# A hybrid encoder trunk on one core: sink columns copied a period later, the first token tile transformed ahead in the Fourier layer, four weight loads placed a product later

## The chip, the cores and the metric

The kernel runs on one NeuronCore of a Trainium2 chip. Five engines work at once, each through its own list of instructions in order: TensorE (PE, matmuls and transposes; its weight loads are shown apart as PEld), VectorE (DVE), ScalarE (ACT), GpSimd (POOL) and SyncE (SP, which here only issues DMA transfers). They are held together by semaphores. The metric is the device time of one execution in microseconds (us); lower is better. The kernel before took 1605.82 us, the median of three runs (1604.63 to 1607.87).

## The reference

Two sequences, of 2048 and of 512 tokens with 1024 channels, go through an attention layer and a Fourier layer, each in the form x + (branch * silu(gate)) @ w_out, and a last RMSNorm.

```python
def banded_gqa_with_sink(q, k, v, rel_bias, sink):      # 16 heads of 64, 4 KV heads
    ...                                                 # 128-query blocks, 3 key blocks
    scores = jnp.einsum('bnqhgd,bnkhd->bnhgqk', qb, kw) * scale + bias
    scores = jnp.where(mask, scores, -jnp.inf)          # |i - j| <= 128
    m = jnp.maximum(jnp.max(scores, axis=-1, keepdims=True), sk)
    p = jnp.exp(scores - m)
    denom = jnp.sum(p, axis=-1, keepdims=True) + jnp.exp(sk - m)
    return einsum(p / denom, v)

def fourier_layer(x, g, w_gate, w_out):
    h = rmsnorm(x, g)
    hg = h.reshape(b, s, 4, 256)
    f = jnp.fft.fftn(hg, axes=(1, 3), norm="ortho").real.reshape(b, s, d)
    return x + (f * jax.nn.silu(h @ w_gate)) @ w_out
```

`sk` is a learned sink logit of each head. All is float32.

## The kernel before, in words

**Precision.** Each float32 operand of a matmul is split in two parts: ACT casts it (the high part), and DVE or POOL subtracts that from it (the low part). A product is then three matmuls (`matmul3`, whose instructions all stand at L94).

**The attention layer** works through five chunks of 512 tokens: chunk 0 is the short sequence, chunks 1 to 4 the long one. A chunk has eight head pairs p, and each pair four query blocks b. The loop over n = 0 to 16 does half a pair in each of its periods: in period n the scores of blocks 2(n%2) and 2(n%2)+1 of pair n//2, beside the transposes (L509), the copies of the transposed probabilities `pts` (L517 on ACT, L518 on DVE) and the products with the values `av` (L535) of the half pair before. Between these, PE does the projections q and g of later pairs (`qp`, `gp`). In chunk 0 the weights come as plain float32 and are split on the way (`load_w`, L110, L113, L118); later chunks load them split.

The order on PE, ACT and DVE in this loop is written out by hand: `seq` and `pe` chain each instruction behind the one before it on its engine. What is not chained (the splitting of weights, DMA issues) is placed by a planner in the compiler by its own costs. A planner also hands out the slots of each pool of tiles, and a transfer into a slot waits until the last reader of the old tile is done.

Per pair there is a bias tile `bt`, tagged `bias`, with two slots. `start()` of a pair, called at the head of an even period for the pair that comes next, loads columns 1 to 384 of it (L426, 384 KB) and has ACT copy the sink logit into its first and last column (L431, 128x4). `biased()` (L470) adds the tile to the scores in PSUM and takes the row's extreme in the same instruction; `exps()` (L478) takes the exponentials. The scores go to three fixed banks `spt[0..2]`: block b of a period uses spt[0] and spt[1], block b+1 uses spt[2] and spt[0], so PE's second group of scores needs that the first bias addition of the same period has read spt[0].

`extra(i)`, i from 4n to 4n+3, adds work to a period: statistics of the next chunk (`stats`: loads of token rows `xs` at L169 and ACT Squares at L161, chained on ACT for the chunks after chunk 1, begun at i = 38 with one step for each even i), and sums of the Fourier layer's weights.

**The Fourier layer** begins with pairs of token tiles of 128 tokens. For a pair, tiles are transposed (`turn`, L972, one PSUM bank for each of the two halves), split (`own`, L979 and L980), summed with each other (`sums`, L995 and L1002) and the sums split (`parts`, L913 and L914), since the gate projection is done with fewer products of sums of blocks (`gates`: products `W`, `Z`, `X`). The channel transform of the first tile of a pair is `z` (24 matmuls from the tile's own split halves, evacuated at L1022), that of the second tile `z_odd_even` (L1036, from the split sum and difference of its halves, evacuated at L1043 and L1044). The first pair is handled ahead of the loop, right behind the attention layer's last output projection; `build(k)` then splits weights for the later products (`wN`, `wT`).

**The end of the kernel** makes output pairs one after the other in `products`, which calls three hooks: `split_g` after the first product, `transform` after the second, `turns` after the fifth. `gated` loads the gate rows `s2` (one by SP, L1240, the mirrored ones by a gather on POOL, L1243), `f_sums` loads weight sums (L1433), 4 transfers of 512 KB.

Of the kernel before, what the change touches and what calls it, by code (L numbers as in the profile page):

```python
# [19 lines left out]
P = 128  # L20
# [22 lines left out]
def encoder(  # L43
# [97 lines left out]
    def attention_phase():  # L141

        with ExitStack() as es:
# [274 lines left out]
            def attention(c, p, res, uTs):  # L418
# [3 lines left out]
                st = {}  # L422

                def start():
                    bt = ap.tile([P, 2, 386], F32, tag="bias", bufs=2, name=f"b{c}_{p}")
                    SP.dma_start(  # L426
                        bt[:, :, 1:385],
                        bass.AP(rowd.tensor, rowd.offset + p * 1024, [[1, P], [512, 2], [1, 384]]),
                    )

                    ends = ACT.copy(bt[:, :, 0:386:385], sk[:, 2 * p : 2 * p + 2, None].to_broadcast([P, 2, 2]))  # L431
                    if p:
                        seq(ACT, ends)
                    st["bias"] = bt
                    uT = wp.tile([P, 2, CH], F32R, align_bytes=LINE, tag="uT", bufs=8, name=f"uT{c}_{p}")
                    uTs.append((uT[:, 0], uT[:, 1]))
                    st["uT"] = uT

                def span(b):
                    gb = tok // P + b  # L440
# [123 lines left out]

                    return split

                return start, scores, biased, exps, divide, transp, parts, av, out_evac

            def out_proj(c, uTs):
                tok = CHUNKS[c][0]  # L570
# [56 lines left out]
                steps.append(lambda: evac(1))  # L627
                return steps

            Heads = namedtuple("Heads", "start scores biased exps divide transp parts av out_evac")  # L630

            def pieces(out, a, b, op):

# [133 lines left out]
            for c in range(len(CHUNKS)):  # L767

                if c > 1:
                    hs, halo = make_h(c, invb)  # L770
                for s in tail:
                    s()
                if c == 1:
                    hs, halo = make_h(c, invb)
                if c:
                    invb0 = kv_proj(c, hs, halo)
                else:
                    invb0 = kv_proj(c, hs, halo, first_norms, early)
                rowd, sk = bias
                uTs = []  # L780
                res = [{} for p in range(8)]
                at = [Heads(*attention(c, p, res[p], uTs)) for p in range(8)]
                loads, work = [], []
                for p in range(8):
                    load, steps = qg_proj(c, p, hs, res[p], invb0)
                    loads.append(load)
                    work += steps
                loads[0]()
                at[0].start()

                ahead_n = 16 if c == 0 else 12
                chain.pop(PE, None)
                for s in work[:8]:
                    s()
                loads[1]()
                for s in work[8:ahead_n]:
                    s()

                m = 15 * KD - ahead_n
                quota = [m * (i + 1) // 27 - m * i // 27 for i in range(27)] + [4, 4]  # L800
                assert sum(quota) == len(work) - ahead_n
                work = work[ahead_n:]
                op = out_proj(c, uTs)
                split = None

                def extra(i):
                    nonlocal norm_steps, invb, inv
                    if c + 1 < len(CHUNKS):
                        if i == 24:
                            norm_steps = stats(c + 1)  # L810
                        if i >= (38 if c else 24) and i % (2 if c else 4) == 0 and norm_steps:
                            inv = norm_steps.pop(0)()
                        elif i == 56:
                            invb = spread(c + 1, inv)
                    if c in EXTRA and i in EXTRA[c]:
                        EXTRA[c][i]()
                    if c == len(CHUNKS) - 1 and i in AHEAD:
                        AHEAD[i]()
                    if c == 0 and i % 8 == 3 and 1 <= i // 8 < 3:
                        load_w(0, LATE[i // 8 - 1], f"late{i // 8}", late=last_exp[0])  # L820

                fourth = bank(f"s{c}")
                zeros(fourth)
                for n in range(17):
                    new = (at[n // 2], 2 * (n % 2)) if n < 16 else None
                    old = (at[(n - 1) // 2], 2 * ((n - 1) % 2)) if n else None
                    if n % 2 == 0 and n < 14:
                        at[n // 2 + 1].start()
                    if n % 2 and n // 2 + 2 < 8:
                        loads[n // 2 + 2]()  # L830
                    chain.setdefault(PE, None)

                    if new:
                        new[0].scores(new[1], spt[:2])
                    if old:
                        for b in range(2):
                            old[0].transp(old[1] + b)
                    if new:
                        for j in range(2):
                            new[0].biased(new[1], j)  # L840
                        new[0].scores(new[1] + 1, (spt[2], spt[0] if n else fourth))
                    if n == 15:

                        for j in range(2):
                            new[0].biased(new[1] + 1, j)
                    if old:
                        for b in range(2):
                            old[0].parts(old[1] + b)
                    if new:
                        for j in range(2):  # L850
                            new[0].exps(new[1], j)
                    if split and c:
                        split()
                        split = None
                    if new:
                        if n < 15:
                            for j in range(2):
                                new[0].biased(new[1] + 1, j)
                        while late:
                            late.pop()()  # L860
                        new[0].divide(new[1], 0)
                        for j in range(2):
                            new[0].exps(new[1] + 1, j)
                        new[0].divide(new[1], 1)
                        for j in range(2):
                            new[0].divide(new[1] + 1, j)
                    for i in range(quota[2 * n] if n < 15 else 18 - n):
                        (work or op).pop(0)()
                    if split:
                        split()  # L870
                        split = None
                    if old:
                        old[0].av(old[1])
                        split = old[0].out_evac(old[1])
                    for i in range(4 * n, 4 * n + 4):
                        extra(i)
                    if n == 16:
                        split()
                    half = quota[2 * n + 1] if n < 14 else 4 if n == 14 else 2
                    for i in range(half):  # L880
                        (work or op).pop(0)()
                chain.pop(PE)
                if c == len(CHUNKS) - 1:

                    for i in range(2):
                        op[i]()
                        op[i] = lambda: None
                tail = op
            return tail

    def fourier_phase(tail):
        with ExitStack() as es:
# [307 lines left out]
            kept = []  # L1200

            pr = pairs[0]
            turns1(pr)
            turns2(pr)
            turns3(pr)
            turns4(pr)
            more()
            more()
            pr.z_odd_even()
            for hf in range(2):  # L1210
                pr.z(hf)
            for k in range(4):
                build(k)
            for n, pr in enumerate(pairs[:-1]):
# [391 lines left out]
            for k1, k2 in ((7, 3), (3, 5), (5, None)):  # L1606
                name, tiles = f"p{k1}", pair(k1, 16, 0)
                gl, tb = nxt["r"]

                def split_g():  # L1610
                    nxt["s"] = [gated(name, r, xtile) for r in tiles]
                    if not ft["N4"]:

                        f_sums("N4", left)
                    nxt["p"] = [halves_of(name, *gl, hf) for hf in range(2)]

                def transform(third):
                    nxt["o"] = Outs(k1, position(name, k1, None, None, tiles, (nxt["s"], tb), nxt["p"], third))

                def turns():  # L1620
                    nxt["o"].operands()
                    nxt["o"].load()
                    if k2:
                        nxt["r"] = reads(k2)

                o.products((split_g, transform, turns))
                o = nxt["o"]
# [102 lines left out]
```

## Time and profile before

| what | us |
| --- | --- |
| median of three runs | 1605.82 |
| the profiled execution | 1608.11 |
| its span, first to last instruction | 1606.3 |
| PE busy in the span | 1586.9 (99%) |
| PEld | 1322.6 (82%) |
| DVE | 1141.7 (71%) |
| ACT | 880.3 (55%) |
| POOL | 438.2 (27%) |

The granted TensorE clock was 0.997 of full speed over the span. The transfers moved 373.90 MB, 233 GB/s. The chain of work that ended last is PE for 83%, DMA for 7%, DVE for 5%, ACT for 2%.

How to read it: times are from the span's start. A row of the view in order of time gives start, duration, engine, line, operation, tiles written and read (`out<-in`), form, and count of merged instructions; in brackets the idle time of the engine before it and what ended that. Matmuls overlap in the pipeline, so that a duration is longer than the distance of two starts, and a busy PE isn't PE at its peak. Idle time of an engine costs only where another waits for it.

### The profile page before, as it was taken

The numbers are of one execution on the slowest core, as the hardware profiler recorded it, in microseconds if no ns is written. First come the engines' busy times: TensorE is split into PE (matmuls) and PEld (weight loads), VectorE is DVE, ScalarE is ACT, GpSimd is POOL, SyncE is SP. The second block draws the span as 40 slices with busy tenths as digits, with TensorE's granted clock in tenths as the row PEclk, the third lists the DMA queues.
The fourth block names the chain that finished last, engine by engine and source line by source line (L and its number), as shares of the span: only waits on it lengthen the run. The fifth ranks groups of instructions, "written<-read, shape, count | busy, mean of one in ns | idle before, by whom it ended". The sixth has DMA issues, their size and how long they took to land.

```text
span 1606.3 us, 27426 instructions
## 1 busy us (share of the span) xinstructions
PE 1586.9 (99%) x9755; PEld 1322.6 (82%) x9755; DVE 1141.7 (71%) x2779; ACT 880.3 (55%) x2107; POOL 438.2 (27%) x605
## 2 busy tenths in 40 slices
PE   9999999999999999999999999999999999999998
PEld 7776888888898888988888888878888887888886
DVE  6787665777538776377764577668878877888696
ACT  6687634677237674257752476646655554343352
POOL 2466561421403414024222242211112121100010
PEclk9999999999999999999999999999999999999999
DMA  7577696655765576756659656656657569455952
GB/s 291 207 286 263 226 349 233 227 220 205 289 230 191 206 257 235 251 194 229 238 164 334 211 208 222 243 201 225 217 203 248 184 224 407 166 185 206 352 192 92
DMA packets 100580, 373.90 MB, mean 233 GB/s; under 512 B 12139, under 2 KB 22379, under 8 KB 83036
## 3 DMA queue, kind: packets, MB, share of 16 engines
q1 hardware_dynamic: 81708, 297.91, 52.4%
q0 software_dynamic: 16400, 70.04, 11.3%
q10 hardware_dynamic: 2336, 4.20, 0.7%
q8 instruction: 78, 1.28, 0.3%
q14 instruction: 58, 0.48, 0.1%
HBM read 280.84 MB, written 91.26 MB: 232 GB/s over the span
## 4 chain that ended last, share of the span: by engine, by line
PE 83%; DMA 7%; DVE 5%; ACT 2%; issue 1%; POOL 1%; SPq 0%; POOLq 0%; DVEq 0%; ACTq 0%
PE qp L94 13%; PE gp L94 12%; PE op L94 9%; PE spt L94 8%; PE spt L451 6%; PE av L535 6%; PE W L94 5%; PE fo L94 4%; PE vp L94 4%; PE pt L509 3%; PE Z L94 3%; PE Wo L94 2%; PE X L94 1%; PE z L94 1%; DMA b<-rowd 1%
## 5 line engine op out<-in xcount | busy, mean ns | idle before, releaser
L470 DVE CUSTOM_DVE_ANT_0 S<-spt,b 128x385 f32<-128x385 f32 (+1 forms) x315 | 154.2, 528 | 121.1 <-PE spt L451 120.8
L94 PE MATMUL qp<-h,wq 128*128 128x512 f32 x960 | 238.6, 398 | 0.0
L94 PE MATMUL gp<-h,wg 128*128 128x512 f32 x960 | 237.4, 395 | 0.0
L94 PEld LDWEIGHTS gp<-h,wg 128*128 128x128 f32 x960 | 174.9, 188 | 43.3 <-issue 9.7
L94 PEld LDWEIGHTS qp<-h,wq 128*128 128x128 f32 x960 | 175.9, 189 | 41.8 <-issue 5.5
L478 ACT ACTIVATE S<-S 128x385 f32<-128x385 f32 (+1 forms) x320 | 190.3, 606 | 18.4 <-DVE S L470 17.0
L517 ACT CAST pts<-pt 128x384 fp32r<-128x384 f32 (+1 forms) x320 | 123.8, 472 | 131.1 <-PE pt L509 130.8
L518 DVE TENSOR_TENSOR pts<-pt,pts 128x384 fp32r<-128x384 f32 (+1 forms) x320 | 147.6, 523 | 34.5 <-ACT pts L517 33.6
L94 PE MATMUL op<-wo,uT 128*128 128x512 f32 x600 | 140.4, 391 | 0.0
L94 PE MATMUL fo<-wo,tTu 128*128 128x512 f32 x576 | 139.1, 392 | 0.0
L94 PEld LDWEIGHTS op<-wo,uT 128*128 128x128 f32 x600 | 111.9, 188 | 23.9 <-issue 0.7
L451 PE MATMUL spt<-kwin,qab 64*128 64x384 f32 (+1 forms) x945 | 129.5, 356 | 0.0
L559 POOL TENSOR_TENSOR uT<-o,uT 128x256 fp32r<-128x256 f32 x75 | 55.6, 741 | 250.5 <-ACT uT L558 246.2
L94 PEld LDWEIGHTS fo<-wo,tTu 128*128 128x128 f32 x576 | 106.3, 188 | 20.3
L535 PEld LDWEIGHTS av<-pts,v 128*128 128x128 f32 x576 | 101.0, 188 | 24.0 <-ACT pts L517 3.7
L535 PE MATMUL av<-pts,v 128*128 128x512 f32 (+1 forms) x576 | 117.0, 342 | 3.3 <-ACT pts L517 2.6
L451 PEld LDWEIGHTS spt<-kwin,qab 64*128 64x128 f32 x945 | 84.2, 185 | 29.9 <-issue 21.5
L490 DVE TENSOR_SCALAR S<-S 128x384 f32<-128x384 f32 (+1 forms) x192 | 91.4, 476 | 6.4
L555 POOL TENSOR_TENSOR o<-o,s 128x256 f32<-128x256 f32 x75 | 55.3, 738 | 134.4 <-DVE o L553 134.1
L94 PE MATMUL spt<-wo,uT 128*128 128x512 f32 x360 | 86.7, 392 | 0.0
L94 PEld LDWEIGHTS spt<-wo,uT 128*128 128x128 f32 x360 | 66.5, 188 | 13.7
L509 PEld LDWEIGHTS pt<-ident,S 64*128 64x128 f32 x1792 | 68.2, 138 | 5.2 <-issue 2.3
(317 smaller groups left out, 2985.8 us busy)
## 6 DMA issues: line engine op xcount, KB each, us to landing
wo<-wsd SPq DMA_DIRECT2D x32, 1024.0 KB, 5.9
wq<-wsd SPq DMA_DIRECT2D x31, 1024.0 KB, 7.6
wg<-wsd SPq DMA_DIRECT2D x31, 1024.0 KB, 5.1
x<-x1d SPq DMA_DIRECT2D x40, 512.0 KB, 3.7
b<-b21d SPq DMA_DIRECT2D x40, 512.0 KB, 6.5
b<-rowd SPq DMA_DIRECT2D x40, 384.0 KB, 4.3
xs<-in_x_dram SPq DMA_DIRECT2D x23, 512.0 KB, 6.7
s2d<-gt POOLq DMA_DIRECT2D x40, 256.0 KB, 3.2
```

What stands on the lines that cost most here:

```text
L94: pe(PE.matmul(out, a[i], b[j], start=start and i + j == 0, stop=stop and i == 1, skip_group_check=more))
L451: pe(PE.matmul(banks[j][:, 2 + k0 * P : 2 + k1 * P], res["q"][rows, qp, b * P : (b + 1) * P], kwin[g][rows, kp, b * P + k0 * P : b * P + k ...
L470: seq(DVE, DVE.tensor_tensor_reduce(out=s[:, e0:e1], in0=ps[:, 1 + e0 : 1 + e1], in1=st["bias"][:, j, 386 - e1 : 386 - e0][:, ::-1], scale ...
L478: last_exp[0] = seq(ACT, ACT.activation(s[:, e0:e1], s[:, e0:e1], AF.Exp, bias=s[:, 386:387], scale=-1.0, accum_out=s[:, 387:388]))
L490: seq(DVE, DVE.tensor_scalar(s[:, ks], s[:, ks], den, None, ALU.mult))
L509: pe(PE.transpose(ps[h][:, kb, j, :], ss[j][rows, 1 + kb * P : 1 + (kb + 1) * P], ident[rows, rows]))
L517: seq(ACT, ACT.copy(hi, ps[:, k0:k1]))
L518: seq(DVE, DVE.tensor_tensor(lo, ps[:, k0:k1], f32(hi), ALU.subtract))
L535: pe(PE.matmul(to, v, pt, start=n == part == 0, stop=part == 1 and n in (1, len(todo) - 1), skip_group_check=n > 1,))
L555: eng.tensor_tensor(o, o, s, ALU.mult)
L559: low = eng.tensor_tensor(lo, o, f32(hi), ALU.subtract)
```

## The change

Three moves; no instruction is added or removed.

1. The copy of the sink columns leaves `start()` and becomes a step of its own, `sinks()`. For pair 0 of a chunk it follows `start()` as before. For pair n//2 + 1 it is called at the end of each odd period n below 15, behind that period's extra work, where `start()` of the same pair was called at the head of period n - 1. The copy is still chained on ACT.
2. For the first pair of the Fourier layer, both halves of the first tile are transposed and split, and `z` of it is done, ahead of the second tile's transposes and sums. In the old order `z` came last.
3. The four loads of `N4` go from `split_g` to the head of `transform`, one product later in the text of the program.

```diff
 def start():
     bt = ap.tile([P, 2, 386], F32, tag="bias", bufs=2, ...)
     SP.dma_start(bt[:, :, 1:385], ...)
-    ends = ACT.copy(bt[:, :, 0:386:385], sk[:, 2 * p : 2 * p + 2, None].to_broadcast([P, 2, 2]))
-    if p:
-        seq(ACT, ends)
     st["bias"] = bt
...
+def sinks():
+    ends = ACT.copy(st["bias"][:, :, 0:386:385], sk[:, 2 * p : 2 * p + 2, None].to_broadcast([P, 2, 2]))
+    if p:
+        seq(ACT, ends)
...
 at[0].start()
+at[0].sinks()
...
     for i in range(4 * n, 4 * n + 4):
         extra(i)
+    if n % 2 and n < 15:
+        at[n // 2 + 1].sinks()
...
 pr = pairs[0]
+for hf in range(2):
+    pr.turn(0, hf)
+for hf in range(2):
+    pr.z(hf)
 turns1(pr)
-turns2(pr)
+for i in (2, 4):
+    pr.sums(i)
+pr.parts(1)
+pr.parts(2)
 turns3(pr)
 turns4(pr)
 more()
 more()
 pr.z_odd_even()
-for hf in range(2):
-    pr.z(hf)
...
 def split_g():
     nxt["s"] = [gated(name, r, xtile) for r in tiles]
-    if not ft["N4"]:
-        f_sums("N4", left)
     nxt["p"] = [halves_of(name, *gl, hf) for hf in range(2)]

 def transform(third):
+    if not ft["N4"]:
+        f_sums("N4", left)
     nxt["o"] = Outs(k1, position(...))
```

`turns1` transposes the second tile, makes its first sum and the split difference; `turns2` was the transposes of the first tile with sums 2 and 4 and parts 1 and 2; `turns3` and `turns4` are part 4, and sum 3 with its part.

More of the change, by code (lines that the diff above doesn't have):

```diff
@@ L437, in start @@
                     st["uT"] = uT
+                def sinks():
+                    ends = ACT.copy(
+                        st["bias"][:, :, 0:386:385], sk[:, 2 * p : 2 * p + 2, None].to_broadcast([P, 2, 2])
+                    )
+                    if p:
+                        seq(ACT, ends)
                 def span(b):
@@ L565, in out_evac @@
                     return split
-                return start, scores, biased, exps, divide, transp, parts, av, out_evac
+                return start, sinks, scores, biased, exps, divide, transp, parts, av, out_evac
             def out_proj(c, uTs):
@@ L628, in out_proj @@
                 return steps
-            Heads = namedtuple("Heads", "start scores biased exps divide transp parts av out_evac")
+            Heads = namedtuple("Heads", "start sinks scores biased exps divide transp parts av out_evac")
             def pieces(out, a, b, op):
@@ L1611, in split_g, with transform @@
                     nxt["s"] = [gated(name, r, xtile) for r in tiles]
+                    nxt["p"] = [halves_of(name, *gl, hf) for hf in range(2)]
+                def transform(third):
                     if not ft["N4"]:
                         f_sums("N4", left)
-                    nxt["p"] = [halves_of(name, *gl, hf) for hf in range(2)]
-                def transform(third):
                     nxt["o"] = Outs(k1, position(name, k1, None, None, tiles, (nxt["s"], tb), nxt["p"], third))
```

## The prediction

> **What bounds the kernel.** I read first the busy time by stage (stretches of the span, one per attention chunk). Columns: the stretch, its length, then for PE, PEld, DVE, ACT and POOL the busy time and the number of instructions, then the granted TensorE clock, the DMA share and GB/s.
>
> ```profile
> 0.00:250.00 250.00, 243.79 (x1523) 197.81 (x1524) 171.38 (x510) 162.22 (x371) 127.26 (x180) 0.99 0.73 269
> 250.00:463.00 213.00, 213.00 (x1424) 177.30 (x1424) 135.85 (x410) 118.52 (x319) 62.30 (x77) 1.00 0.65 235
> 463.00:679.00 216.00, 216.00 (x1465) 180.89 (x1464) 143.49 (x414) 124.08 (x324) 61.89 (x77) 1.00 0.64 227
> 679.00:888.00 209.00, 209.00 (x1406) 173.74 (x1405) 136.89 (x402) 118.45 (x307) 61.49 (x80) 1.00 0.65 233
> ```
>
> In chunks 1 to 3 PE is never idle: nothing can be won there, and whatever holds PE is lost in full. In chunk 0 it is idle for some 6 us. Then I asked what the sink copy (L431) waits for (us, times):
>
> ```profile
>   DMA b<-rowd: 55.6, 32
> ```
>
> These 55.6 us are ACT's. They cost only where PE then waits, so I looked through ACT's and PE's instructions in order of time for such places. There are two, both in chunk 0. Columns: start, duration, engine, line, operation, tiles, form, count, idle before and what ended it.
>
> ```profile
> 130.85 0.20 ACT L431 COPY b<-sk 128x4 f32<-128x4 f32 x1 [3.63 <-DMA b<-rowd]
> 131.07 1.41 ACT L517 CAST pts<-pt 128x384 fp32r<-128x384 f32 x4
> ...
> 137.88 1.04 ACT L113 CAST wq<-w32q 128x1024 fp32r<-128x1024 f32 x1
> ...
> 151.10 0.20 ACT L431 COPY b<-sk 128x4 f32<-128x4 f32 x1 [4.49 <-DMA b<-rowd]
> ...
> 152.26 1.41 ACT L517 CAST pts<-pt 128x384 fp32r<-128x384 f32 x4
> ```
> ```profile
> 127.73 1.02 PE L509 MATMUL pt<-ident,S 64*128 64x64 f32 x20
> ...
> 132.54 0.51 PE L535 MATMUL av<-pts,v 128*128 128x512 f32 x1 [0.81 <-ACT pts L517]
> 133.32 1.20 PE L535 MATMUL av<-pts,v 128*128 128x512 f32 x5 [0.28 <-DVE pts L518]
> ...
> 139.07 0.56 PE L509 MATMUL pt<-ident,S 64*128 64x64 f32 x11 [0.80 <-DVE o L553]
> ...
> 153.73 0.50 PE L535 MATMUL av<-pts,v 128*128 128x512 f32 x1 [1.82 <-ACT pts L517]
> 154.52 1.19 PE L535 MATMUL av<-pts,v 128*128 128x512 f32 x5 [0.28 <-DVE pts L518]
> ```
>
> Last, the clock. It fell to half in two stretches, each of which begins right after a long wait of PE:
>
> ```profile
> 155.78:159.19 3.41, 3.41 (x10) 2.63 (x9) 2.89 (x12) 3.26 (x7) 1.69 (x4) 0.50 0.86 216
> ...
> 1080.79:1084.21 3.42, 3.42 (x15) 3.03 (x14) 2.66 (x5) 1.91 (x6) 0.00 (x0) 0.50 0.95 380
> ```
>
> Half the clock for 3.41 us loses 3.41 / 2 = 1.7 us.
>
> **Part 1, the sink columns: what is won in chunk 0.** The copy goes from the head of an even period to the end of the odd period behind it, some 9 us after its load was issued. Its own 0.20 us stays. At 130.85 the next work, the copies of the transposed probabilities, could begin when the transposes end, 127.73 + 1.02 = 128.75, not at 131.07: 2.3 us sooner, so the waits of 0.81, 0.28 and, in the backlog, 0.80 go (1.9). At 151.10 the waits of 1.82 and 0.28 go (2.1), and with them the half clock (1.7). Together 5.7. What is late next: ACT would come to the cast of wq 2.3 us before 137.88, and its load was issued, and took from issue to landing (us, the last number), as here:
>
> ```profile
> 126.38 0.33 SPq L110 DMA_DIRECT2D w32q<-in_w_in_dram  x1
> ```
> ```profile
> w32q<-in_w_in_dram SPq DMA_DIRECT2D x1, 512.0 KB, 10.7
> ```
>
> that is until 137.1, so ACT keeps only 0.8 of the 2.3, and PE, 1.9 ahead, waits about 1.1 for the casts behind it. I take 5.7 - 1.1 = **4.6 won**; bounds 2.1 (only the waits at 153.73) and 5.7. In the other chunks and periods this costs and wins nothing: PE is busy throughout.
>
> **Part 1, what the copy now stands behind.** The new place is behind the extra work of the odd period in ACT's written order, and the columns are needed by the first bias addition (L470) of the very next period, where before there were two periods between. In period 11 of chunks 1 to 3 that extra work is two Squares of the next chunk's statistics, chained on ACT, and the second waits for its rows to land. Below, for each of these chunks: that Square, the first bias addition of period 12, and PE's second group of scores of period 12.
>
> ```profile
> 367.66 1.06 ACT L161 ACTIVATE xs<-xs 128x1024 f32<-128x1024 f32 x1 [2.17 <-DMA xs<-in_x_dram]
> ...
> 581.77 1.06 ACT L161 ACTIVATE xs<-xs 128x1024 f32<-128x1024 f32 x1 [2.15 <-DMA xs<-in_x_dram]
> ...
> 796.98 1.06 ACT L161 ACTIVATE xs<-xs 128x1024 f32<-128x1024 f32 x1 [2.36 <-DMA xs<-in_x_dram]
> ```
> ```profile
> 367.15 0.43 DVE L470 CUSTOM_DVE_ANT_0 S<-spt,b 128x257 f32<-128x257 f32 x1 [1.76 <-PE spt L451]
> ...
> 581.41 0.56 DVE L470 CUSTOM_DVE_ANT_0 S<-spt,b 128x385 f32<-128x385 f32 x1 [1.90 <-PE spt L451]
> ...
> 796.42 0.56 DVE L470 CUSTOM_DVE_ANT_0 S<-spt,b 128x385 f32<-128x385 f32 x1 [1.91 <-PE spt L451]
> ```
> ```profile
> 367.67 0.77 PE L451 MATMUL spt<-kwin,qab 64*128 64x384 f32 x6
> ...
> 581.93 0.89 PE L451 MATMUL spt<-kwin,qab 64*128 64x384 f32 x6
> ...
> 796.94 0.89 PE L451 MATMUL spt<-kwin,qab 64*128 64x384 f32 x6
> ```
>
> The copy starts when the Square ends and takes 0.20; then the addition runs (0.43 or 0.56); only then is the bank spt[0] free, which the second matmul of PE's group writes, some 0.15 us into the group. Chunk 1: 367.66 + 1.06 + 0.20 + 0.43 = 369.35, less 367.82, is 1.5 us of waiting. Chunk 2: 583.59 - 582.08 = 1.5. Chunk 3: 798.80 - 797.09 = 1.7. Behind the waiting matmul stand the whole projection and all later PE work, in written order; so **4.7 lost**. Nothing catches it up, as PE has no other wait in these chunks. Bounds: 0 if the rows landed over 1.7 us sooner, and 5.3 with 0.2 more of semaphore time each.
>
> **The clock after these waits.** A wait of 1.82 + 0.28 was followed by 3.41 us at half clock, the waits of 0.81 + 0.28 at 132.54 were not. 1.5 to 1.7 lies between, nearer to the upper. No row shows where the limit is; for each wait I give a chance of three in ten, and one drop of the three is then likeliest: **1.7 lost**; bounds 0 and 5.1.
>
> [...]
>
> **Part 2, the head of the Fourier layer.** Eight transposes and 24 matmuls of the first tile go ahead, with two ACT casts, two DVE subtractions and two evacuations; no DMA is moved, but the first output tile now takes the first slot of the memory just vacated, ahead of the two weight loads, which may shift those on SP's queue a little either way.
>
> ```profile
> 1075.96 1.91 PE L972 MATMUL trb<-ident,x 128*128 128x128 f32 x16
> 1079.69 0.50 PE L1036 MATMUL z<-chan_sb,S 128*128 128x256 f32 x2 [1.82 <-ACT S L913]
> ...
> 1086.96 3.03 PE L94 MATMUL z<-chan_sb,tTb 128*128 128x256 f32 x24
> ...
> 1103.45 0.50 PE L94 MATMUL W<-wT,S 128*128 128x512 f32 x1 [0.18 <-ACT wT L913]
> ```
> ```profile
> 1077.60:1088.00 10.40, 8.36 (x42) 7.09 (x41) 8.78 (x15) 6.61 (x15) 0.08 (x1) 0.84 0.79 269
> 1088.00:1092.60 4.60, 4.60 (x30) 4.11 (x29) 2.35 (x6) 3.85 (x9) 1.10 (x2) 1.00 0.98 327
> 1092.60:1104.80 12.20, 12.02 (x65) 10.15 (x64) 12.18 (x20) 9.20 (x18) 0.00 (x0) 1.00 0.58 219
> ```
>
> PE now waits 1.82 for the odd tile's sums and then loses 1.7 to the clock: 3.5 in all. The 24 matmuls (3.03) fill that wait, so it goes. But DVE has not a tenth of a us free from 1092.60 to 1104.80, and PE at 1103.45 waits already for the last weights that DVE splits there. A PE that is 3.5 earlier waits for DVE, unless DVE too comes sooner; it was idle for 1.6 and 2.25 us before, behind ACT and behind the loads of the next rows. I take half of these as moved, 2.0: **2.0 won**; bounds 3.5 won and 2.0 lost (rival below).
>
> **Part 3, the last weight sums.** Four loads (N4, 2 MB) are placed one product later.
>
> ```profile
> 1523.39 1.22 DVE L1294 TENSOR_TENSOR up<-up,s2p 128x1024 f32<-128x1024 f32 x1 [3.10 <-DMA s2p<-s2d,mir]
> ...
> 1524.76 1.50 PE L1337 MATMUL tr<-ident,up 128*128 128x128 f32 x12 [1.21 <-DVE up L1294]
> ```
> ```profile
> 1512.63 1.93 SPq L1433 DMA_DIRECT2D fN<-fN4d  x4
> ```
>
> PE waits 1.21 us here for gate rows that are gathered while the N4 loads run. But between the old place and the new one the code issues nothing on SP and nothing on POOL: SP's order stays, and the loads wait for slots, not for the product. I take **0**; bounds 1.2 won, and 0.5 lost if N4 came late for its product.
>
> **Sum:** -4.6 + 4.7 + 1.7 - 2.0 + 0 = -0.2 us. Against the profiled execution (1608.11, a span of 1606.3 and 1.8 around it) that is 1607.9; it ran 2.3 above the median of the runs, 1605.82, against which the forecast is **1605.6**.
>
> **Rivals.** *The columns hold nobody* (faster): the rows of the Square land in time, or DVE is not reached by it. Then -4.6 - 2.0 = -6.6, 1599.2. For it: chunks 0 and 4 have no such chain. Against: three chunks of three show 2.15 to 2.36 us of waiting for these rows. *The odd tile waits for a bank* (slower): there are five banks in this pool; two hold the first tile's transposes until its sums are done, two take its products, one the first half of the odd tile; if the second half must wait until a product is evacuated, the sums start behind the 24 matmuls, 3.0 us later, of which I let DVE's idle time before 1088 take 1.0, and DVE's closed run ends 2.0 later. Then -4.6 + 4.7 + 1.7 + 2.0 = +3.8, 1609.6. It decides from 3.4 us of change at the head. Against: PE ran all 16 transposes in one piece before, so what is ready may again go first. *Part 3 does what it says*: 1.2 less, 1604.4. *No clock is lost*: 1.7 less, 1603.9; both stay inside the forecast's band.
>
> **Chances.** 0.2%, 3.2 us, is about what a measurement of this kernel can tell from no change (its three runs span 3.2). Forecast with its two small variants 0.42; columns hold nobody, or the head and the tail give all, 0.31; bank, or three clock drops with a weaker chunk 0, 0.27. Range: down to the first rival with a little of the head's bound, 1598.5; up to the second with one more drop, 1611.5. The forecast's own range is 1602.6 to 1608.8.
>
> **What would show it.** Right: L431 waits for no b load; no PE wait and no half clock between 130 and 160; in chunks 1 to 3 the first L470 of period 12 waits for ACT's L431, and PE's scores behind it for 1.5 us; odd-tile products at the head without a wait, but a later one for wT; fN still issued right behind s2p. Wrong: PE at 100% in chunks 1 to 3, or a wait of PE among the head's transposes.

## The result, and the profile after

| | us |
| --- | --- |
| forecast | 1605.6 (1598.5 to 1611.5) |
| before, median beside the changed kernel | 1605.58 |
| changed kernel, median of four runs | 1615.68 (1612.88 to 1619.24) |
| ratio | 1.0062, 95% interval 1.0039 to 1.0085 |
| profiled execution of the changed kernel | 1612.88, span 1611.1 |

The change makes the kernel slower, by 0.4 to 0.9%. A second comparison on another chip gave 1.0060 (1.0042 to 1.0078). The profiled execution is the fastest of its four.

I read the profile after in the order of the prediction. First the busy time by stage; columns as before.

```profile
0.00:250.00 250.00, 246.38 (x1554) 201.54 (x1555) 173.95 (x515) 163.16 (x375) 127.23 (x180) 1.00 0.74 273
250.00:463.00 213.00, 211.79 (x1408) 176.21 (x1407) 136.84 (x412) 118.68 (x320) 61.73 (x77) 1.00 0.65 232
463.00:679.00 216.00, 214.49 (x1450) 179.19 (x1450) 140.81 (x410) 122.13 (x318) 62.25 (x77) 1.00 0.63 226
679.00:888.00 209.00, 206.53 (x1368) 170.49 (x1368) 134.95 (x396) 117.12 (x303) 61.41 (x80) 0.99 0.64 228
```

Chunk 0 has 2.6 us more of PE's work in the same 250 us, and each of chunks 1 to 3, which had no idle PE, now has 1.2, 1.5 and 2.5 us of it. What chunk 0 won is seen where the first `gp` product behind it begins, in order of time: before, then after.

```profile
258.18 1.52 PE L94 MATMUL gp<-h,wg 128*128 128x512 f32 x6
```
```profile
140.85 1.80 PE L539 MATMUL av<-pts,v 128*128 128x512 f32 x6 [0.68 <-ACT pts L521]
...
150.99 1.30 PE L539 MATMUL av<-pts,v 128*128 128x512 f32 x6
...
253.33 1.98 PE L94 MATMUL gp<-h,wg 128*128 128x512 f32 x8
```

That is 258.18 - 253.33 = 4.85 us, with the half clock at 155.78 gone. What the copy (now L437) waits for and who waits for it (us, times):

```profile
  DMA b<-rowd: 7.3, 5
who waited for it (us, times):
  DVE S L474: 17.6, 6
```

It waits for loads only in its five calls for pair 0, one in each chunk. In exchange DVE's bias addition (now L474) waits for the copy. The place in each of chunks 1 to 3: ACT's Square, the copy, DVE's addition, PE's second group of scores (now L455), whose first matmul has gone and whose other five wait.

```profile
363.02 1.06 ACT L161 ACTIVATE xs<-xs 128x1024 f32<-128x1024 f32 x1 [2.04 <-DMA xs<-in_x_dram]
...
364.08 0.18 ACT L437 COPY b<-sk 128x4 f32<-128x4 f32 x1
...
579.50 1.06 ACT L161 ACTIVATE xs<-xs 128x1024 f32<-128x1024 f32 x1 [2.34 <-DMA xs<-in_x_dram]
...
797.73 1.06 ACT L161 ACTIVATE xs<-xs 128x1024 f32<-128x1024 f32 x1 [3.29 <-DMA xs<-in_x_dram]
```
```profile
364.29 0.43 DVE L474 CUSTOM_DVE_ANT_0 S<-spt,b 128x257 f32<-128x257 f32 x1 [3.41 <-ACT b L437]
```
```profile
364.78 0.79 PE L455 MATMUL spt<-kwin,qab 64*128 64x384 f32 x5 [1.21 <-DVE S L474]
...
581.39 0.78 PE L455 MATMUL spt<-kwin,qab 64*128 64x384 f32 x5 [1.51 <-DVE S L474]
...
799.62 0.90 PE L455 MATMUL spt<-kwin,qab 64*128 64x384 f32 x5 [2.47 <-DVE S L474]
```

With what the matmul that straddles the wait loses, PE stands 1.5, 1.8 and 2.7 us later behind these places. Behind the third the clock is halved for one stretch, over which PE loses another 1.6 us:

```profile
800.15:803.56 3.41, 3.41 (x10) 2.48 (x8) 3.34 (x12) 3.04 (x10) 0.73 (x1) 0.50 0.29 97
```

The next difference is small and in nearly every even period. Here is one of chunk 1: PE's first scores, its second scores, and DVE's first bias addition; before, then after.

```profile
330.52 0.62 PE L451 MATMUL spt<-kwin,qab 64*128 64x256 f32 x6
...
331.70 0.77 PE L451 MATMUL spt<-kwin,qab 64*128 64x384 f32 x6
```
```profile
331.18 0.43 DVE L470 CUSTOM_DVE_ANT_0 S<-spt,b 128x257 f32<-128x257 f32 x1 [1.75 <-PE spt L451]
```
```profile
325.96 0.62 PE L455 MATMUL spt<-kwin,qab 64*128 64x256 f32 x6
...
327.14 0.85 PE L455 MATMUL spt<-kwin,qab 64*128 64x384 f32 x6
```
```profile
326.72 0.42 DVE L474 CUSTOM_DVE_ANT_0 S<-spt,b 128x257 f32<-128x257 f32 x1 [1.86 <-issue]
```

The addition starts 0.76 us behind PE's first scores where it was 0.66, though ACT's copy had been done 2.7 us before; it is put down to no engine, but to issue. PE's second scores need the bank that this addition reads, have no slack, and take 0.08 longer. Outside the three big waits PE so falls back by 0.4 to 0.7 us in each of chunks 1 to 4, 2.2 in all.

Last the head of the Fourier layer (transposes now at L979, the evacuation of `z` at L1029, casts at L986, the low parts of the tiles at L987), PE, then ACT, then DVE:

```profile
1080.87 1.03 PE L979 MATMUL trb<-ident,x 128*128 128x128 f32 x8
1082.14 0.74 PE L94 MATMUL z<-chan_sb,tTb 128*128 128x256 f32 x4 [0.24 <-ACT tTb L986]
1082.72 0.49 PE L979 MATMUL trb<-ident,x 128*128 128x128 f32 x3
1082.96 2.64 PE L94 MATMUL z<-chan_sb,tTb 128*128 128x256 f32 x20
1085.44 0.71 PE L979 MATMUL trb<-ident,x 128*128 128x128 f32 x5
...
1096.11 1.20 PE L94 MATMUL W<-wT,S 128*128 128x512 f32 x4 [1.00 <-ACT c L1096]
1097.87 1.09 PE L979 MATMUL trb<-ident,x 128*128 128x128 f32 x8 [0.56 <-DVE x L971]
...
1109.07 0.73 PE L94 MATMUL W<-wT,S 128*128 128x512 f32 x2 [0.54 <-DVE wT L921]
```
```profile
1084.68 0.65 ACT L1029 ACTIVATE z<-z 128x512 f32<-128x512 f32 x1 [2.10 <-PE z L94]
```
```profile
1087.26 0.69 DVE L987 TENSOR_TENSOR tTb<-trb,tTb 128x512 fp32r<-128x512 f32 x1 [3.85 <-ACT tTb L986]
```

The wait of 1.82 us and the half clock are gone. But the last five transposes of the odd tile run only at 1085.44, when ACT has evacuated the first `z` (1084.68 + 0.65): in the trace the weight load of the second of the five, with which the tile's second half begins, waits for a semaphore of ACT, and that of no transpose ahead of it does. DVE sits idle for 3.85 us before it has anything of the odd tile. PE then waits behind it: 1.00, 0.56, 0.54 and two more of 0.2 and 0.56. PE's first transpose is 4.91 us behind the kernel before (1080.87 against 1075.96), and PE is 5.12 behind it once the head is over: +0.2, no gain. The 4.91 is, up to rounding, what stands above: 6.0 of waits, 1.6 of clock and 2.2 of small steps, less 4.85.

At the end PE's wait ahead of the last products is 1.38 where it was 1.21; the N4 loads still go out right behind the gate rows.

```profile
1529.56 1.50 PE L1349 MATMUL tr<-ident,up 128*128 128x128 f32 x12 [1.38 <-DVE up L1306]
```

### The profile page after: what moved, and what is told of

Its sections match the earlier page's. It is cut to its first block, busy times and chain, and to the rows that moved or that the text cites. A ratio compares the mean times of both kernels' runs of the same rounds, so it can differ in the third digit from the quotient of the medians.

```text
span 1611.1 us, 27438 instructions
## 1 busy us (share of the span) xinstructions
PE 1588.5 (99%) x9755; PEld 1322.7 (82%) x9755; DVE 1140.3 (71%) x2779; ACT 879.3 (55%) x2107; POOL 436.4 (27%) x605
## 3 DMA queue, kind: packets, MB, share of 16 engines
q8 instruction: 78, 1.28, 0.3%
## 4 chain that ended last, share of the span: by engine, by line
PE 85%; DMA 4%; issue 4%; DVE 3%; ACT 3%; POOL 1%; SPq 0%; POOLq 0%; DVEq 0%; ACTq 0%
PE gp L94 13%; PE qp L94 13%; PE op L94 9%; PE spt L94 8%; PE spt L455 7%; PE av L539 6%; PE W L94 5%; PE fo L94 4%; PE vp L94 4%; PE pt L513 3%; PE Z L94 2%; PE Wo L94 2%; PE z L94 1%; PE X L94 1%; DMA xs<-in_x_dram 1%
## 5 line engine op out<-in xcount | busy, mean ns | idle before, releaser
L474 DVE CUSTOM_DVE_ANT_0 S<-spt,b 128x385 f32<-128x385 f32 (+1 forms) x315 | 154.2, 528 | 136.9 <-PE spt L455 83.6
L455 PE MATMUL spt<-kwin,qab 64*128 64x384 f32 (+1 forms) x945 | 133.5, 358 | 5.2 <-DVE S L474 5.2
L455 PEld LDWEIGHTS spt<-kwin,qab 64*128 64x128 f32 x945 | 86.0, 185 | 37.3 <-issue 24.0
```

What stands on the lines that cost most here:

```text
L455: pe(PE.matmul(banks[j][:, 2 + k0 * P : 2 + k1 * P], res["q"][rows, qp, b * P : (b + 1) * P], kwin[g][rows, kp, b * P + k0 * P : b * P + k ...
L474: seq(DVE, DVE.tensor_tensor_reduce(out=s[:, e0:e1], in0=ps[:, 1 + e0 : 1 + e1], in1=st["bias"][:, j, 386 - e1 : 386 - e0][:, ::-1], scale ...
```

## The experiments

All are against the kernel before, whose runs on the same chip had medians of 1606.6 to 1607.2 us. The differences are those of the ratio, times 1607 us; the plain difference of two medians, which some of the expectations use, lies up to 1.1 us off that. All kernels compute the whole result.

| kernel | median, us | difference, us (95%) |
| --- | --- | --- |
| columns alone | 1611.48 | +5.8 (+3.5 to +8.0) |
| head alone | 1607.88 | +0.3 (-1.1 to +1.8) |
| N4 loads alone | 1606.50 | -1.0 (-2.6 to +0.5) |
| columns, copy ahead of the extra work | 1605.41 | -1.3 (-2.7 to +0.2) |
| columns, copy at the head of the odd period | 1603.55 | -3.2 (-4.7 to -1.8) |
| only pair 6 of chunks 1 to 3 late | 1612.74 | +6.7 (+4.7 to +8.8) |
| head, only `z` moved | 1608.49 | +2.1 (+0.6 to +3.7) |
| head, all transposes first | 1604.25 | -3.1 (-4.5 to -1.8) |
| the whole change again | 1615.53 | +9.6 (+6.7 to +12.5) |
| columns and head | 1613.76 | +6.4 (+4.2 to +8.7) |
| columns and N4 loads | 1611.90 | +4.8 (+2.9 to +6.9) |
| the whole, copy ahead of the extra work | 1606.80 | +0.3 (-1.1 to +1.8) |
| both good placings together | 1601.48 | -5.1 (-7.1 to -3.2) |

**The three parts alone.** Each part of the diff was applied by itself to the kernel before.

> Part 1 alone: the sink columns are copied at the end of the odd period, head and last weight sums as before. Theory A (the loss is all part 1's): -4.9 us in chunk 0, three waits of PE in period 12 of chunks 1 to 3 of 1.5, 1.8 and 2.7 us (+6.0), one stretch at half clock behind them (+1.7), and a second wait of the first bias addition in the other even periods, which starts it and PE's second scores 0.1 us later each time (+1.8 over the chunks): +4.6 us, 1610. Theory B (part 1 as I forecast it, the rest of the loss comes from the head or the weights): -4.6 + 4.7 + 1.7 = +1.8, 1607.4.

> Part 2 alone: the first token tile is transformed ahead at the head of the Fourier layer. Theory A (the odd tile's second half waits for a bank until the first product is evacuated, and its sums start later): what the wait of 1.82 us and the half clock gave back is lost again behind the later sums, +0.4 us, 1606.0. Theory B (the head gains as forecast and only what part 1 did in front of it hid that): -2.0 us, 1603.6.

> Part 3 alone: the four loads of N4 stand one product later in the program. Theory A (nothing stands between the old and the new place on the queues): 0 us, 1605.6, and the wait of PE ahead of the last products stays at 1.2 to 1.5 us. Theory B (the gathers of the gate rows come sooner): -1.2 us and that wait gone.

The loss is part 1's. In its profile PE waits 1.38, 1.28 and 1.39 us at the three places and no stretch at half clock follows; that execution took 1608.06, the fastest of five, and the others, at a lower mean clock, 1611.27 to 1614.23. The head alone moves nothing that can be measured, with the same late transposes: DVE sits idle for 3.87 us there. The N4 loads move nothing either (PE's wait behind them 1.01).

**Where the copy stands.** Two other places for the same call: ahead of the odd period's extra work, and at the head of the odd period. Both edits are shown against the columns alone.

```diff
+if n % 2 and n < 15:
+    at[n // 2 + 1].sinks()
 for i in range(4 * n, 4 * n + 4):
     extra(i)
-if n % 2 and n < 15:
-    at[n // 2 + 1].sinks()
```
```diff
+if n % 2 and n < 15:
+    at[n // 2 + 1].sinks()
...
 if new:
     new[0].scores(new[1], spt[:2])
...
     extra(i)
-if n % 2 and n < 15:
-    at[n // 2 + 1].sinks()
```

> Part 1 alone, with the copy called ahead of the odd period's extra work instead of behind it. Theory A (two separate costs: the Square that the copy stood behind, and a second wait of the first bias addition on ACT's fresh copy): the three waits of PE and the half clock behind them go, the 0.1 us at each pair stays: -4.9 + 1.8 = -3.1 us, 1602.5. Theory B (only the Square costs): -4.9 us, 1600.7, and PE's second scores start as early as before. Theory C (the bias addition waits for ACT whatever stands ahead of the copy): waits of 1 us and more stay, 1605 or above.

> Part 1 alone, with the copy called at the head of the odd period: half a pair's work behind the load, half a pair's work ahead of the first use. Theory A (load landed, no Square ahead of the copy, and the bias addition finds ACT's copy long done, so that it needs no wait of its own): chunk 0 gains its 3.1 us of waits, 4.9 in runs in which the half clock followed them, and nothing is given back: 1602.6, and the second scores of a period start as early as before. Theory B (the second wait stays because the copy is nearer than before): 1605.4, as with the copy ahead of the extra work. Theory C (the load has not landed yet in chunk 0): 1606.7.

In both, no PE wait for the addition is left in period 12. Between the two lies the small second cost. Groups of instructions by form, over chunks 1 to 3: the bias addition and the scores (busy us, mean ns; idle time before them and what ended it), for the copy ahead of the extra work, then at the head of the odd period.

```profile
L474 DVE CUSTOM_DVE_ANT_0 S<-spt,b 128x385 f32<-128x385 f32 x173 | 89.4, 555 | 70.6 <-PE spt L455 47.2 <-issue 19.5 <-ACT b L437 4.0
...
L455 PE MATMUL spt<-kwin,qab 64*128 64x384 f32 x519 | 75.4, 368 | 0.0
```
```profile
L474 DVE CUSTOM_DVE_ANT_0 S<-spt,b 128x385 f32<-128x385 f32 x173 | 89.4, 554 | 68.3 <-PE spt L455 68.3
...
L455 PE MATMUL spt<-kwin,qab 64*128 64x384 f32 x519 | 73.6, 366 | 0.0
```

With the copy ahead of the extra work 19.5 us of DVE's waits in front of the addition are put down to issue, and 4.0 to the copy; with the copy at the head of the period all is PE's, as before, and the scores have their old 73.6 us. The two differences in the table are 1.9 us apart, and these rows give 1.8. So it isn't the time of the copy that counts here (it is long done in both cases when the scores are), but whether DVE still has something to wait for besides PE. The semaphores in the traces show this: with the copy ahead of the extra work, 21 bias additions of chunks 1 to 3, one for each of seven pairs in each chunk, wait for a semaphore of ACT; with the copy at the head of the period, and in the kernel before, none does. Why none needs to is argued from the code: in the odd period DVE waits for later work of ACT anyhow (`divide` for the exponentials), and a copy ahead of that is then known to be done.

**The hold by itself.** Only the copies of pair 6 in chunks 1 to 3 go behind the Squares; all others stand where the kernel before has them. The edit against the columns alone:

```diff
 at[n // 2 + 1].start()
+if n != 10 or not 0 < c < 4:
+    at[n // 2 + 1].sinks()
...
     extra(i)
-if n % 2 and n < 15:
-    at[n // 2 + 1].sinks()
+if n == 11 and 0 < c < 4:
+    at[6].sinks()
```

> The kernel before, with a single copy moved: that of pair 6 in chunks 1 to 3, to the end of period 11, behind the two Squares. Nothing is won in chunk 0, no other pair gets a second wait. Theory A (the hold is real and stands by itself): three waits of PE of 1.5 to 2.7 us, about 5.1, and about one stretch at half clock more: +5 to +8.5, 1613.5. Theory B (the waits cost little, the loss of part 1 is the second waits of all the other pairs): +2 or less, 1608.7.

Three moved copies of 0.2 us each cost 6.7 us (4.7 to 8.8). PE's waits, in order of time:

```profile
370.52 1.13 PE L455 MATMUL spt<-kwin,qab 64*128 64x384 f32 x5 [1.38 <-DVE S L474]
...
587.98 0.79 PE L455 MATMUL spt<-kwin,qab 64*128 64x384 f32 x5 [1.39 <-DVE S L474]
...
806.09 0.79 PE L455 MATMUL spt<-kwin,qab 64*128 64x384 f32 x5 [1.19 <-DVE S L474]
```

Here the clock was halved behind the first two, not behind the third.

**The head.** First only `z` was moved, with transposes and sums in the old order; then the changed order with one step put back, the odd tile's transposes ahead of `z`.

```diff
 turns3(pr)
 turns4(pr)
+for hf in range(2):
+    pr.z(hf)
 more()
 more()
 pr.z_odd_even()
-for hf in range(2):
-    pr.z(hf)
```
```diff
 for hf in range(2):
     pr.turn(0, hf)
+turns1(pr)
 for hf in range(2):
     pr.z(hf)
-turns1(pr)
 for i in (2, 4):
     pr.sums(i)
```

> The kernel before with another order at the head of the Fourier layer: transposes, sums and their splitting in the old order, the odd tile first, and only the 24 matmuls of the first tile put ahead of the second tile's. Theory A (the head's gain was lost only because the odd tile waited for a bank): the wait of 1.82 us is filled and the sums come as early as before: -1 to -2 us, 1605.2. Theory B (DVE bounds the stretch behind it, so that an earlier PE waits there): 1606.7, with the waits for wT and S grown by what the first wait gave.

> The kernel before, with the changed head but for one step: all 16 transposes go first, the odd tile's too, and the first tile's 24 matmuls behind them. So the odd tile's transposes have four free banks and wait for no evacuation. Theory A (the head's gain was lost to the bank): the odd tile's sums start within 2 us of the last transpose, DVE has no idle time of 3 us and more there, the waits for wT and x behind it are as before, and the waits of 1.82 and 0.22 us are filled: -1.5 us, 1605.3. Theory B (whatever the order, DVE and ACT bound this stretch): 1606.5 to 1608, with waits for wT, x and s of 0.2 to 0.6 us behind it.

Moving `z` alone costs 2.1 us, more than either theory had: the first tile is then split behind the odd tile's work, the compiler's planner puts `z` first on PE all the same, and PE waits longer than before for the cast. In order of time, first that kernel, then the one with all transposes first:

```profile
1080.55 0.74 PE L94 MATMUL z<-chan_sb,tTb 128*128 128x256 f32 x4 [3.01 <-ACT tTb L979]
```
```profile
1075.24 1.91 PE L972 MATMUL trb<-ident,x 128*128 128x128 f32 x16
1076.90 0.96 PE L94 MATMUL z<-chan_sb,tTb 128*128 128x256 f32 x5
1077.70 0.39 PE L94 MATMUL W<-wB,tTb 128*128 128x512 f32 x1
1077.93 2.44 PE L94 MATMUL z<-chan_sb,tTb 128*128 128x256 f32 x19
...
1101.41 0.48 PE L1036 MATMUL z<-chan_sb,S 128*128 128x256 f32 x2 [0.45 <-DVE s L1002]
```

All 16 transposes run in one piece, the 24 matmuls follow without a wait, and behind them one wait of 0.45 is left. The gain of 3.1 us is more than the 2.0 I had forecast for the head, and it hangs on one call: the idea of part 2 was good, and its order took it away.

**The whole once more.** The parts sum to 5.8 + 0.3 - 1.0 = +5.1, the whole costs +9.6. So it was run again, two pairs of its parts were run, the whole was profiled twice more and columns with head once more, and the whole was run with the copy ahead of the extra work.

> The changed kernel once more, on a chip that also runs its parts. The parts alone gave, against 1606.7 us: columns +4.7, head +1.1, weights -0.2 us. Theory A (they add up): +5.6, 1612.3. Theory B (they don't: columns and head together cost more, as the first comparison says): 1615 to 1616.

> Columns and head, without the N4 loads. The whole change cost 8.7 us where its parts sum to 5.6. Theory A (columns and head together make the difference: the rows of the Square land 1 us later in chunk 3, and where the waits fall decides the half clock): the wait of PE in chunk 3 is 2.5 us or more, with half clock behind it, 1614 to 1616. Theory B (they add up and the N4 loads make the difference): wait in chunk 3 of 1.8 us, 1612.5.

> Columns and N4 loads, without the head. Theory A (as in the run of columns and head): wait in chunk 3 of 1.8 us, +4.7, 1611.5. Theory B (the N4 loads make the difference): 2.5 us or more in chunk 3, 1613 to 1615. Theory C (which way the wait in chunk 3 goes is chance from run to run): anything between.

> The whole change, one more profile. Theory A (the late landing of the rows in chunk 3 belongs to this build): ACT waits 3.2 us or more for the rows of the second Square in chunk 3, PE 2.4 or more behind it, with half clock in the next window. Theory B (chance from run to run): a wait of ACT of 2.0 to 2.4 us and of PE of 1.1 to 1.4, as in columns alone, columns with head, and columns with N4.

> As the look before: A 3.2 us or more for the rows in chunk 3, B 2.0 to 2.4 us. Of the clock: a window of 3.41 us with 1.7 us or more of idle PE is followed by half clock, one with less than 1.35 us isn't; between the two either may come.

> Columns and head without the N4 loads, a second profile. Theory A (the late rows belong to the build of the whole change): 2.0 to 2.4 us of waiting for the rows in chunk 3, as in its first profile. Theory B (chance): either, 3.2 us or more among them.

> The whole change with one step undone: the copy is called ahead of the odd period's extra work, so that no Square stands in front of it. Theory A (all that the whole change costs beyond its head is the hold and the clock behind it): no wait of PE for the bias addition in chunks 1 to 3 whenever the rows land, -1.3 us for the columns as alone, +1.1 for the head: 1606 to 1607. Theory B (the three parts together cost something that is not in the hold): 1609 or more.

The late rows in chunk 3 come by chance. The whole change showed ACT waiting 3.29, 3.39, 2.08 and 2.31 us for them in four profiles, columns and head 2.06 and 2.27; the kernel with the copy at the head of the odd period had 3.23 too, and lost 0.8 us there instead of 2.7 and more. In the first profiles of columns with head and of columns with N4 PE waits 1.21 and 1.16 us in chunk 3, so neither pair of parts makes the rows late. In order of time, the wait of PE in the second and the third profile of the whole:

```profile
801.70 1.29 PE L455 MATMUL spt<-kwin,qab 64*128 64x384 f32 x5 [2.58 <-DVE S L474]
```
```profile
800.46 0.79 PE L455 MATMUL spt<-kwin,qab 64*128 64x384 f32 x5 [1.26 <-DVE S L474]
```

The third and the fourth profiled execution of the whole took 1612.87 and 1610.85 us, the second profile of columns and head 1613.25. With the copy ahead of the extra work the whole change is level with before, which is the sum of its pieces (-1.3 + 0.3 - 1.0 = -2.0) within the intervals: what it loses, it loses by the hold. Whether the whole costs more than its parts isn't settled. The interval of the sum, about 2 to 8 us if the three errors are independent, overlaps that of the whole, 6.7 to 12.5. The runs of the whole have a mean clock of 0.9962 against 0.9974 to 0.9980 for columns alone and with either other part, and 0.001 of 1610 us is 1.6, so that by an estimate from these means some 2 to 3 us of the excess stand in the clock; in which places can't be seen, as only one execution of each comparison left a trace.

**Both good placings.** The copy at the head of the odd period and all transposes first, N4 as before:

> The copy at the head of the odd period, together with that order of the head (all transposes first); the N4 loads as before. Theory A (both are gains): 1603.5 - 1.5 = 1602.0. Theory B (the head gives nothing): 1603.5 to 1604.5.

It took 1601.48 us, ratio 0.9968 (0.9956 to 0.9980), and is faster than both kernels. In its profile chunks 1 to 3 are full again and between the first and the last 10 us there is no stretch at half clock.

```profile
250.00:463.00 213.00, 213.00 (x1418) 177.20 (x1417) 137.47 (x414) 119.22 (x323) 61.70 (x77) 1.00 0.66 236
463.00:679.00 216.00, 216.00 (x1461) 180.70 (x1460) 142.69 (x413) 122.92 (x322) 62.23 (x77) 1.00 0.64 228
679.00:888.00 209.00, 209.00 (x1406) 173.79 (x1405) 134.79 (x399) 116.65 (x301) 61.88 (x80) 1.00 0.65 233
```

## Why the prediction was wrong

The forecast lies 10.1 us below the median. Half of that is between the two profiled executions: they differ by 1612.88 - 1608.11 = +4.8, where the sum gave -0.2. Four steps failed: the small cost of the even periods was put at nothing, the hold was sized too small, the gain at the head did not come, and the step from profile to median counted something twice.

- **What is won in chunk 0: right.** 4.85 against 4.6. The wait for the late casts that I took off is there too, 0.68 us at 140.85.
- **What the copy now stands behind: right in mechanism.** Square, copy, addition, bank and scores stand as forecast in all three chunks, and the kernel with only pair 6 moved shows it alone. Sizes 1.5, 1.8 and 2.7 against 1.5, 1.5 and 1.7: the term was too small by 1.3, and 1.0 of that is chunk 3, where I took the landing of the rows from one execution. The steps between the engines took 0.03 us from the copy's end to the addition and 0.06 from the addition's end to the scores, 0.09 in each of the three chunks, where the upper bound had 0.2.
- **"In the other chunks and periods this costs and wins nothing": wrong.** This is the step that failed unseen. Nearly every even period now starts its bias addition 0.1 us later, PE has no slack there, and 2.2 us are gone over chunks 1 to 4; with the copy at the head of the odd period the scores have their old time again.
- **The clock: right in count, wrong in kind.** One stretch came, as forecast, and that was luck: the other three profiles of the changed kernel have two, one and none. Nor did it go by the length of a wait: 1.82 us at the head were followed by half clock in the kernel before and not in the columns alone, as the section on the hardware shows.
- **The head: wrong.** "The 24 matmuls fill that wait, so it goes" came true, and the 2.0 us did not. The rival of the bank did: +0.2 in place of -2.0, a miss of 2.2, not the +2.0 that I had priced for it, since the half clock went as well. What I held against it (all 16 transposes ran in one piece before) said nothing of an order in which the products stand between them; the sign that I had named for being wrong, a wait of PE among the head's transposes, is there (0.24). The doubt about DVE was right in direction and too strong: with all transposes first, DVE too comes sooner, and 3.1 are won.
- **Part 3: right.** Nothing.

Together: 2.2 + 1.3 + 2.2 - 0.25 for chunk 0 - 0.1 for the clock = 5.35. Behind the head 0.35 of that is made up (5.12 there, 4.77 between the two spans), which leaves 5.0. The other half is the step from profile to median. I took 2.3 us off because the profiled execution of before ran that much above its median; but part of what it had more were its two stretches at half clock, which my sum had already spent as gains (1.7 in chunk 0, 1.7 at the head). The other runs of the kernel before agree: of the 27 beside the parts alone, the eight with a mean clock of 0.999 have a median of 1605.96 us, the eleven with 0.997, the clock of the profiled execution, one of 1607.91. The profiled execution after runs 2.8 below its own median. 2.3 + 2.8 = 5.1. The slowest of the other three runs after had a mean clock of 0.993 against 0.997; why the other two, at 0.997 too, took 1.9 and 3.7 us more than the profiled one isn't shown.

## What to carry to other kernels

A copy of 0.2 us, chained on its engine, took on here the waits of the Square ahead of it (2.04, 2.34 and 3.29 us): ask what it stands behind, and how far ahead of its first use it is; one period earlier, at the head of the odd period in place of its end, was worth 9 us here (-3.2 against +5.8). Where PE, which set the pace, had no slack, a consumer that got one more thing to wait for cost time though that thing was done, and it showed only as 0.1 us in nearly every even period, 2.2 us in all. When work is put into a gap, look at what must still be issued to open the next stage, and put that first: with the odd tile's transposes behind the products the head gave +0.3 us, with them ahead -3.1.

## What the runs showed of the hardware

**The half clock came in windows of 3.41 us.** In 18 profiles, every stretch at half clock between 20 and 1590 us lasts 3.41 us, 16 of them in all, and within one execution all stretches start at multiples of 3.413 us from each other. In the second profile of the whole change:

```profile
583.31:586.72 3.41, 3.41 (x10) 2.67 (x9) 3.21 (x13) 2.73 (x9) 0.73 (x1) 0.50 0.53 205
801.77:805.18 3.41, 3.41 (x10) 2.54 (x11) 3.37 (x12) 3.04 (x11) 0.73 (x1) 0.50 0.41 126
```

801.77 - 583.31 is 64 times 3.4133; the two of before, 155.78 and 1080.79, are 271 times that apart. I laid this grid over each trace and added up PE's idle time in each of the 8261 windows. Nine windows had 1.79 us or more: half clock in the next window all nine times. Twenty had 1.38 to 1.68: seven times. None of the others, 1.36 or less, was followed by it. What decided among those twenty isn't shown. In the kernel before, the window from 152.37 held 1.65 us of the waits at 153.73 and 154.52, and the window from 1077.38 held 2.04 us of those at 1079.69 and 1080.41; half clock followed both, 3.41 us at 0.50, by an estimate 3.41 / 2 = 1.7 us each. In the changed kernel the window from 796.74 had 2.47 and was followed by it, that from 578.28 had 1.51 and was not. In the columns alone the wait of 1.82 us at the head was cut in two by the grid (1.23 and 0.81 idle, the small wait behind it included) and kept its clock. The place of the grid is not the same in each run: its first window begins 2.18 us into the span in the kernel before, 1.43 in the changed kernel, 3.04 in its second profile. A grid that moves would fit the scatter: the runs of a kernel with such waits lie 4.1 us (only pair 6 late) to 8.5 us (the whole again) apart, those with both good placings 2.9. That the windows make the scatter isn't shown, as few executions left a trace.

**The landing of a load.** The 512 KB of rows in front of the Square landed 5.0 to 5.5 us after issue in most profiles of chunk 3, and 6.35 and 6.45 us after it in the first two profiles of the whole change, with the same order of transfers on SP. With the copy at the head of the odd period the Square began 6.3 us after that issue. The cause stays open.
